# A Fourier and RG-LRU layer on one core: seven-product (Strassen) output projection for the last three position blocks, x put into PSUM for two others, and a new order of that stage

## The chip, the cores and the metric

The kernel runs on 1 core of one Trainium2 chip. The metric is the device time of one execution in microseconds. TensorE (PE) multiplies, VectorE (DVE) and ScalarE (ACT) work element by element, GpSimd (POOL) issues DMAs in this stage, and so does SyncE (SP), whose queue is in order. Before the change, three runs took 667.74, 668.42 and 664.72 us, the median is 667.74.

## The reference, cut to what matters

One layer of a diffusion backbone on 2048 positions of 1024 channels. The change is in the last step alone, `out_proj` with its gated residual and the final norm:

```python
def out_proj(y_f, g_f, y_l, g_l, w_out):
    y = jnp.concatenate([y_f * jax.nn.silu(g_f), y_l * jax.nn.silu(g_l)], axis=-1)
    return y @ w_out
...
        x = x + gate * out_proj(yf_x, gf_x, yl_x, gl_x, w_out[l])
    return rmsnorm(x, final_gain)
```

`y_f` comes from the Fourier group, `y_l` from the bidirectional recurrence, `g_f` and `g_l` are their gate paths. `gate` is one vector, so the kernel multiplies it into `w_out` once.

## The kernel before

All matrix products are made in three passes: each factor is split into a rounded part (hi) and the rest (lo), and `mm3` (L70 to L73) issues hi x hi, hi x lo and lo x hi into the same PSUM tile. A left factor is the stationary operand of a matmul, the weights are the moving one, so each matmul also loads its stationary tile (PEld).

The stages follow each other: input projection (string S1), Fourier transform and linear map (STEPS), gates and recurrence (S2), and the output projection (S3). Each string is a list of tokens, and its order is the order in which the instructions stand on PE, ACT and DVE (a manual schedule, L732). On SP and POOL the order is left to the scheduler. The last stage works on 8 blocks of 256 positions in the order 0, 3, 4, 7, 1, 2, 5, 6. The weights are in SBUF as `wo[k, n]`: 8 tiles k of 128 rows by 2 column halves n of 512, hi and lo. The tokens of a block b, with the Fourier half q = 0 and the recurrence half q = 1:

- D loads `g` and `yf` or `yl` from DRAM on SP (L946 to L954), A is silu(g) on ACT (L1001), P multiplies on DVE (L1008 for yf in two instructions of 512, L1010 for yl in one of 1024).
- J rounds to hi on ACT (L1015), K subtracts to lo on DVE (L1019); four tiles of 512 in a block.
- X loads x (`xr`, four buffers) on SP (L1055). m is a group of 4 k for position half t and column half n: 12 matmuls of 512 columns into `po` (four PSUM tiles).
- a adds `po` to x on DVE (L1077), b squares and sums on ACT (L1082), r takes the root on ACT (L1086), f is a reciprocal and the scaling with the final gain on DVE (L1090, L1091) and the store from POOL's queue (L1092). x's buffer is free for the next X when that store has ended.

A block without a special form is 2 x 2 x 8 products, 96 matmuls of 512 columns. The last half (Z6.1, `p3_last`) is cut into 512, 256 and 256 columns and is squared, scaled and stored in pieces, its halves from the queues of ACT and SP. The buffers of g, yf, yl and of the hi and lo tiles have the tag q4, 14 of them.

Of the kernel before, what the change touches and what calls it, by code (L numbers as in the profile page):

```python
# [52 lines left out]
def tile_layer(ctx, tc, xp, xnat, xt_in, ctxn, ctxt, w_ada, vec, bgate, fgain, w_in, w_g, w_four, w_gate, w_out,  # L53
# [997 lines left out]
    def p3_x(b):
        xs[b] = []
        for t in range(2):
            x = py.tile([P, D], F32, name=f"xr{b}_{t}", tag="xr", bufs=4)
            nc.sync.dma_start(x, xnat[256 * b + P * t:256 * b + P * t + P, :])  # L1055
            xs[b].append(x)
# [31 lines left out]
    def p3_scale(b, t):  # L1088
        o, st = xs[b][t], s3[b, t]
        nc.vector.reciprocal(out=st[:, 3:4], in_=st[:, 2:3])  # L1090
        nc.vector.scalar_tensor_tensor(out=o, in0=o, scalar=st[:, 3:4], in1=fg_bc, op0=ALU.mult, op1=ALU.mult)  # L1091
        nc.gpsimd.dma_start(out[256 * b + P * t:256 * b + P * t + P], o)  # L1092

    def p3_last(b, t):
        o = xs[b][t]
# [3 lines left out]
        for i, (n0, n1) in enumerate(((0, 512), (512, 768), (768, 1024))):  # L1099
            n, m0 = divmod(n0, 512)  # L1100
            po = ps3.tile([P, n1 - n0], F32, name=f"po{b}_{t}_{n0}", tag="po")
            for k in range(KD):
                p3_mms(po, b, t, n, k, m0, m0 + n1 - n0)
# [135 lines left out]
```

## Time and profile before

| | us |
|---|---|
| median of three runs | 667.74 |
| lowest, highest | 664.72, 668.42 |
| the profiled execution: time | 663.85 |
| its span | 661.7 |
| PE, DVE, ACT, POOL busy in the span | 651.6, 477.2, 402.9, 105.5 |
| block 4's first matmul, PE's last matmul (start) | 521.7, 655.60 |

The profiled execution's time is its span and 2.15 us around it. An engine's busy time says how much work it had, not whether anybody waited for it: that is read from the chain of waits and from the stretch in question. The duration of a matmul row is modelled and overlaps the next, so the pace of PE is read from the starts. The granted TensorE clock was 0.997 of full speed over the span.

### The profile page before, as it was taken

The numbers are of one execution on the slowest core, as the hardware profiler recorded it, in microseconds if no ns is written. First come the engines' busy times: TensorE is split into PE (matmuls) and PEld (weight loads), VectorE is DVE, ScalarE is ACT, GpSimd is POOL, SyncE is SP. The second block draws the span as 40 slices with busy tenths as digits, with TensorE's granted clock in tenths as the row PEclk, the third lists the DMA queues.
The fourth block names the chain that finished last, engine by engine and source line by source line (L and its number), as shares of the span: only waits on it lengthen the run. The fifth ranks groups of instructions, "written<-read, shape, count | busy, mean of one in ns | idle before, by whom it ended". The sixth has DMA issues, their size and how long they took to land.

```text
span 661.7 us, 10718 instructions
## 1 busy us (share of the span) xinstructions
PE 651.6 (98%) x4124; PEld 572.6 (87%) x4124; DVE 477.2 (72%) x771; ACT 402.9 (61%) x578; POOL 105.5 (16%) x170
## 2 busy tenths in 40 slices
PE   8999999999999999999999999999999999999996
PEld 8888888888988898998999999989988888888885
DVE  4768899877656775588699899879988455644513
ACT  5575877556644545959598696797643455543502
POOL 0000101031221204432212221131300000000000
PEclk9999999999999999999999999999999999999998
DMA  8996876539698776436344442251578677774211
GB/s 334 417 395 205 259 266 204 211 104 278 143 314 283 248 241 182 127 89 185 112 144 124 164 155 88 69 175 56 178 254 310 204 240 244 240 261 146 95 64 63
DMA packets 69884, 130.21 MB, mean 197 GB/s; under 512 B 7076, under 2 KB 39972, under 8 KB 69834
## 3 DMA queue, kind: packets, MB, share of 16 engines
q1 hardware_dynamic: 51066, 82.36, 37.9%
q0 software_dynamic: 12384, 39.00, 18.0%
q10 hardware_dynamic: 6384, 8.18, 4.0%
q8 instruction: 32, 0.52, 0.3%
q14 instruction: 18, 0.15, 0.1%
HBM read 91.24 MB, written 38.27 MB: 196 GB/s over the span
## 4 chain that ended last, share of the span: by engine, by line
PE 93%; DMA 3%; ACT 2%; DVE 1%; issue 1%; POOL 0%; SPq 0%; DVEq 0%; ACTq 0%; POOLq 0%
PE po L71 9%; PE pg L71 9%; PE po L72 9%; PE po L73 9%; PE pg L73 9%; PE pg L72 9%; PE pul L71 5%; PE pul L73 4%; PE pul L72 4%; PE ptt L71 2%; PE ptt L73 2%; PE ptt L72 2%; PE pl L72 2%; PE pl L73 2%; PE pl L71 2%; DMA yf_d<-ya 1%
## 5 line engine op out<-in xcount | busy, mean ns | idle before, releaser
L71 PE MATMUL pg<-hg,wg 128*128 128x256 f32 x512 | 144.2, 282 | 0.0
L73 PE MATMUL pg<-hg,wg 128*128 128x256 f32 x512 | 143.7, 281 | 0.0
L72 PE MATMUL pg<-hg,wg 128*128 128x256 f32 x512 | 143.5, 280 | 0.0
L71 PE MATMUL po<-wo,y 128*128 128x512 f32 (+1 forms) x264 | 102.4, 388 | 0.0
L72 PE MATMUL po<-wo,y 128*128 128x512 f32 (+1 forms) x264 | 102.3, 387 | 0.0
L73 PE MATMUL po<-wo,y 128*128 128x512 f32 (+1 forms) x264 | 102.3, 387 | 0.0
L71 PEld LDWEIGHTS pg<-hg,wg 128*128 128x128 f32 x512 | 96.3, 188 | 3.3 <-ACT g L852 1.2
L72 PEld LDWEIGHTS pg<-hg,wg 128*128 128x128 f32 x512 | 96.3, 188 | 0.7
L73 PEld LDWEIGHTS pg<-hg,wg 128*128 128x128 f32 x512 | 96.4, 188 | 0.0
L424 POOL DMA_DIRECT2D g_d<-gs x80 | 57.7, 723 | 135.5 <-DVE gs L758 63.2
L71 PEld LDWEIGHTS po<-wo,y 128*128 128x128 f32 x264 | 49.9, 189 | 11.0
L73 PEld LDWEIGHTS po<-wo,y 128*128 128x128 f32 x264 | 49.6, 188 | 11.2
L72 PEld LDWEIGHTS po<-wo,y 128*128 128x128 f32 x264 | 49.6, 188 | 10.7
L71 PE MATMUL pul<-hl,wu 128*128 128x512 f32 x124 | 49.9, 402 | 0.0
L1082 ACT ACTIVATE j<-xr 128x1024 bf16<-128x1024 f32 x15 | 15.9, 1057 | 55.3 <-DVE xr L1077 55.3
L73 PE MATMUL pul<-hl,wu 128*128 128x512 f32 x124 | 48.9, 395 | 0.0
L72 PE MATMUL pul<-hl,wu 128*128 128x512 f32 x124 | 48.8, 394 | 0.0
L852 ACT ACTIVATE g<-pl,vecs 128x1024 f32<-128x1024 f32 x32 | 35.5, 1116 | 13.5 <-PE pl L73 13.3
L287 ACT ACTIVATE h<-xt,sh,gn 128x512 f32<-128x512 f32 x31 | 25.2, 813 | 19.2 <-DVE gn L149 10.4
L71 PE MATMUL ptt<-wf,eo 128*128 128x260 f32 (+1 forms) x128 | 36.5, 285 | 0.0
L73 PE MATMUL ptt<-wf,eo 128*128 128x260 f32 (+1 forms) x128 | 36.3, 283 | 0.0
L72 PE MATMUL ptt<-wf,eo 128*128 128x260 f32 (+1 forms) x128 | 36.2, 283 | 0.0
(298 smaller groups left out, 1459.6 us busy)
## 6 DMA issues: line engine op xcount, KB each, us to landing
xt<-in_xt_dram SPq DMA_DIRECT2D x16, 512.0 KB, 5.2
blk<-in_w_ada_dram SPq DMA_DIRECT2D x16, 512.0 KB, 9.5
hr<-h_d SPq DMA_DIRECT2D x32, 256.0 KB, 3.7
xr<-in_xnat_dram SPq DMA_DIRECT2D x16, 512.0 KB, 3.7
g<-g_d SPq DMA_DIRECT2D x15, 512.0 KB, 5.5
out_dram<-xr POOLq DMA_DIRECT2D x15, 512.0 KB, 2.9
dm<-in_dct_dram POOLq DMA_DIRECT2D x12, 514.0 KB, 8.2
x<-in_xp_dram SPq DMA_DIRECT2D x12, 512.0 KB, 5.7
```

Source lines behind the costliest of these rows:

```text
L71: nc.tensor.matmul(out_, lh, rh, start=first, stop=False, skip_group_check=skip)
L72: nc.tensor.matmul(out_, lh, rl, start=False, stop=False, skip_group_check=skip)
L73: nc.tensor.matmul(out_, ll, rh, start=False, stop=last, skip_group_check=skip)
L287: nc.scalar.activation(out=h[:, 0:n], in_=x, func=AF.Identity, scale=g, bias=b)
L424: queue.dma_start(dst[:, :, row:row + s1 - s0], s[:, :, P * i - off + s0:P * i - off + s1])
L852: nc.scalar.activation(out=t[:, c0:c0 + cn], in_=pg[:, 0:cn], func=AF.Sigmoid, bias=vecs[:, q:q + 1])
L1082: nc.scalar.activation(out=junk, in_=xs[b][t], func=AF.Square, accum_out=s3[b, t][:, 0:1])
```

## The change

The output projection of blocks 2, 5 and 6 (`ST`) is made by the seven products of Strassen's method in Winograd's form. The y of a block is seen as 2 x 2 (position halves by Fourier and recurrence half), the weights as 2 x 2 (row halves by column halves). For each k of 4, four combinations of weight tiles are formed on the chip once, in float, and split into hi and lo: token Q (`t_raw`, DVE), H (`t_hi`, cast on ACT), L (`t_lo`, DVE). Per block S forms four combinations of y on DVE, h and l split seven left factors, p (`s_mm`) makes a product of 4 k, 12 matmuls of 512 columns, and q (`s_read`) adds a PSUM tile to a half of x, seven times (block 6: six of 512 and two of 256 columns, with its last product in two pieces, p6.8 and p6.9). Products 6, 5 and 3 are added onto the PSUM tile of product 1 after it has been read, product 4 onto that of product 7.

In blocks 7 and 1, token e (`p3_fill`) copies x into the PSUM tile on ACT, the matmuls add onto it without a start flag, token a is gone, and b and f read PSUM.

Besides: q4 has 6 buffers in place of 14; the pool of the stage ahead is closed before the projection's own pool is opened; x is loaded by halves (X b.t); from there on the order on SP and POOL is written by hand too. Both halves of block 6 are finished in pieces (`s_last`): the second half is scaled on ACT as a whole and stored from POOL, the first half last, its two column halves stored from ACT and SP. The tokens of S3 stand in a new order behind block 3's preparation.

```diff
-Q4 = 14
+Q4 = 6
+TR = 2
...
+    manual = tc.manual_schedule(engines={mybir.EngineType.PE, mybir.EngineType.Activation, mybir.EngineType.DVE,
+                                         mybir.EngineType.SP, mybir.EngineType.Pool})
...
             w[:, 0, m0:m1], w[:, 1, m0:m1], k == 0 and (b, t) not in filled, k == KD - 1, skip=True)
...
+    def p3_fill(b, t):
+        filled.add((b, t))
+        pos[b, t] = ps3.tile([P, D], F32, name=f"po{b}_{t}", tag="po")
+        nc.scalar.copy(pos[b, t], xs[b][t])
...
+    def t_raw(k, i):
+        if i != 2:
+            tr[k, i] = py.tile([P, 2, 512], F32, name=f"tr{k}_{i}", tag="tr", bufs=TR)
+        b11, b12, b21, b22 = ([r(wo[k + 4 * a, n][:, e, 0:512]) for e in range(2)] for a in range(2) for n in range(2))
+        w = tr[k, 1 if i == 2 else i]
+        if i % 2:
+            nc.vector.tensor_tensor(out=w, in0=r((wo[k, 1], wo[k + 4, 1])[i // 2][:, :, 0:512]),
+                                    in1=r(wo[k, i // 2][:, :, 0:512]), op=ALU.subtract)
+            nc.vector.tensor_tensor(out=w[:, 0], in0=w[:, 0], in1=w[:, 1], op=ALU.add)
+            return
+        o = w[:, int(i == 2)]
+        nc.vector.tensor_tensor(out=o, in0=(b22, b21)[i // 4][0], in1=tr[k, 1][:, i // 4], op=ALU.subtract)
+        nc.vector.tensor_tensor(out=o, in0=o, in1=(b22, b21)[i // 4][1], op=ALU.add)
...
+    def t_lo(k, i):
+        t = wt[k, i]
+        nc.vector.tensor_tensor(out=t[:, 1, 0:512], in0=tr[k, 1 if i == 2 else i][:, int(i == 2)], in1=r(t[:, 0, 0:512]),
+                                op=ALU.subtract)
...
+    def s_add(b, i):
+        a11, a12, a21, a22, s1 = (s_view(b, c) for c in (1, 2, 7, 4, 5))
+        o, x, y, op = {1: (s1, a21, a22, ALU.add), 2: (a11, s1, a11, ALU.subtract),
+                       3: (a21, a11, a21, ALU.subtract), 4: (a12, a12, a11, ALU.subtract)}[i]
+        nc.vector.tensor_tensor(out=o, in0=x, in1=y, op=op)
...
+    def s_mm(b, c):
+        p = {2: 2, 4: 1, 7: 1, 8: 3, 9: 4}.get(c, 0)
+        if c in (1, 2, 7, 8, 9):
+            pos[b, p] = ps3.tile([P, D], F32, name=f"po{b}_{p}", tag="po")
+        m0, m1, c = (0, 256, 3) if c == 8 else (256, 512, 3) if c == 9 else (0, 512, c)
+        o = pos[b, p][:, 0:m1 - m0]
+        t = yv[b, "s", c]
+        for k in range(4):
+            w = wo[k, 0] if c == 1 else wo[k + 4, c - 2] if c < 4 else wt[k, {4: 4, 5: 1, 6: 2, 7: 3}[c]]
+            mm3(o, t[:, 0, k], t[:, 1, k], w[:, 0, m0:m1], w[:, 1, m0:m1], (c in (1, 2, 7) or p > 2) and k == 0, k == 3, skip=True)
+
+    def s_read(b, i):
+        t, n, p = ((0, 0, 0), (0, 0, 2), (1, 0, 0), (1, 1, 0), (0, 1, 0), (1, 1, 1), (1, 0, 1),
+                   (0, 1, 0), (0, 2, 3), (0, 3, 4))[i]
+        w = 256 if i > 7 else 512
+        src = pos[b, p][:, 0:w]
+        o = xs[b][t][:, 512 + 256 * (n - 2) if i > 7 else 512 * n:][:, 0:w]
+        nc.vector.tensor_tensor(out=o, in0=o, in1=src, op=ALU.add)
...
+        if t:
+            nc.scalar.activation(out=q, in_=q, func=AF.Copy, scale=rs)
+            nc.gpsimd.dma_start(out[t0:t0 + P, :], q)
+            return
```

Three places in the order. First DVE behind the lo splits of block 7 (y_0_7, y_1_7): `tr` are raw combinations of weights, `wo` the weights, `xr` x, `po` PSUM, `s` the norm's scalars. Before:

```order
L1019 TENSOR_TENSOR y_0_7_5861<-g_7_5855,y_0_7_5861 128x512
L1019 TENSOR_TENSOR y_1_7_5864<-g_7_5855,y_1_7_5864 128x512
L1077 TENSOR_TENSOR xr_0_5693<-xr_0_5693,po_0_5867 128x1024
L1090 RECIPROCAL s_4_0_5917<-s_4_0_5917 128x1
L1091 SCALAR_TENSOR_TENSOR xr_0_5693<-xr_0_5693,s_4_0_5917,fg_bc 128x1024
```

After:

```order
L1023 TENSOR_TENSOR y_1_7_5898<-g_7_5820,y_1_7_5898 128x512
L1115 TENSOR_TENSOR tr_1_5920<-wo_1_5187,wo_0_5196 128x1024
L1117 TENSOR_TENSOR tr_1_5920<-tr_1_5920 128x512
L1103 RECIPROCAL s_3_1_5870<-s_3_1_5870 128x1
L1104 SCALAR_TENSOR_TENSOR xr_1_5590<-xr_1_5590,s_3_1_5870,fg_bc 128x1024
L1090 TENSOR_TENSOR xr_0_5865<-xr_0_5865,po_0_5830 128x1024
L1120 TENSOR_TENSOR tr_1_5920<-wo_1_5533,tr_1_5920 128x512
L1121 TENSOR_TENSOR tr_1_5920<-tr_1_5920,wo_1_5533 128x512
```

The combinations of weights stand between the sums and scalings of blocks 3 and 4, each reading what the one before it wrote.

Second DVE after the change at block 2's first reading (`t_2`, `t_3` are lo parts of combined weights, `s_2_...` with `g_2` a left factor of block 2); none of these stood in the kernel before:

```order
L1115 TENSOR_TENSOR tr_3_6368<-wo_1_5544,wo_1_5349 128x1024
L1117 TENSOR_TENSOR tr_3_6368<-tr_3_6368 128x512
L1169 TENSOR_TENSOR xr_0_6283<-xr_0_6283,po_0_6347 128x512
L1129 TENSOR_TENSOR t_2_6240<-tr_1_6184,t_2_6240 128x512
L1150 TENSOR_TENSOR s_2_6361<-g_2_6092,s_2_6361 128x512
L1103 RECIPROCAL s_1_0_6298<-s_1_0_6298 128x1
L1104 SCALAR_TENSOR_TENSOR xr_0_6031<-po_0_6071,s_1_0_6298,fg_bc 128x1024
```

Between the reading of product 1 and the scaling of block 1's first half stand the two lo splits for block 2's third product.

Third SP's queue around the loads of block 5 (`xr` of x, `g_5`, `yf`, `yl`). Before:

```order
L1055 DMA xr_0_6188<-in_xnat_dram 128x1024
L954 DMA g_5_6318<-g_d 128x4x256
L949 DMA yf_6320<-yf_d 128x4x128 x2
L1055 DMA xr_1_6190<-in_xnat_dram 128x1024
L954 DMA g_5_6336<-g_d 128x4x256
L951 DMA yl_6338<-yl_d 128x4x256
```

After:

```order
L1063 DMA xr_0_6283<-in_xnat_dram 128x1024
L1063 DMA xr_1_6363<-in_xnat_dram 128x1024
L956 DMA g_5_6422<-g_d 128x4x256
L951 DMA yf_6424<-yf_d 128x4x128 x2
L1063 DMA xr_0_6428<-in_xnat_dram 128x1024
L956 DMA g_5_6447<-g_d 128x4x256
L953 DMA yl_6449<-yl_d 128x4x256
```

Before, the loads of block 5 stand between those of block 2's x; after, both x loads of block 2 and the first one of block 5 stand ahead of the last g and yl of block 5.

## Rows read from the trace of the kernel before

**Rows 1.** The page's part 4, the chain that ended last, shares of the span.

```profile
PE 93%; DMA 3%; ACT 2%; DVE 1%; issue 1%; POOL 0%; SPq 0%; DVEq 0%; ACTq 0%; POOLq 0%
```

**Rows 2.** Stretches: length, busy (instructions) of PE, PEld, DVE, ACT, POOL; clock, DMA share, GB/s.

```profile
521.70:588.60 66.90, 66.90 (x289) 54.19 (x288) 37.42 (x47) 35.76 (x52) 4.79 (x9) 1.00 0.67 227
588.60:655.90 67.30, 67.27 (x313) 55.32 (x311) 28.60 (x38) 23.66 (x38) 3.19 (x6) 1.00 0.31 111
655.90:661.70 5.80, 0.00 (x0) 0.00 (x0) 1.50 (x4) 1.52 (x4) 0.00 (x0) 0.67 0.23 90
```

**Rows 3.** Timeline of PE near the end: start, duration, line, shapes.

```profile
642.13 0.40 PE L73 MATMUL po<-wo,y 128*128 128x512 f32 x1
...
647.70 0.39 PE L73 MATMUL po<-wo,y 128*128 128x512 f32 x1
...
650.02 0.28 PE L71 MATMUL po<-wo,y 128*128 128x256 f32 x1
...
652.85 0.28 PE L71 MATMUL po<-wo,y 128*128 128x256 f32 x1
...
655.60 0.28 PE L73 MATMUL po<-wo,y 128*128 128x256 f32 x1
```

**Rows 4.** Groups by line and form, 520 to 661.7: busy us, mean ns | idle before.

```profile
L1091 DVE SCALAR_TENSOR_TENSOR xr<-xr,s,fg_bc 128x1024 f32<-128x1024 f32 x15 | 19.3, 1285 | 0.5
L1077 DVE TENSOR_TENSOR xr<-xr,po 128x1024 f32<-128x1024 f32 x14 | 17.0, 1216 | 19.7 <-PE po L73 19.7
L1082 ACT ACTIVATE j<-xr 128x1024 bf16<-128x1024 f32 x15 | 15.9, 1057 | 55.3 <-DVE xr L1077 55.3
L1019 DVE TENSOR_TENSOR y<-g,y 128x512 fp32r<-128x512 f32 x20 | 12.9, 689 | 7.1 <-ACT y L1015 7.1
L1015 ACT CAST y<-g 128x512 fp32r<-128x512 f32 x20 | 11.4, 618 | 13.5 <-DVE g L1010 6.5 <-issue 5.6 <-DVE g L1008 1.4
...
L1008 DVE TENSOR_TENSOR g<-g,yf 128x512 f32<-128x512 f32 x10 | 6.5, 690 | 4.4 <-ACT g L1001 4.4
L1010 DVE TENSOR_TENSOR g<-g,yl 128x1024 f32<-128x1024 f32 x5 | 6.1, 1225 | 1.6 <-ACT g L1001 1.6
...
L1062 ACT ACTIVATE j<-xr 128x512 bf16<-128x512 f32 x1 | 0.6, 631 | 3.6 <-DVE xr L1060 3.6
```

**Rows 5.** Timeline of all engines behind the last matmul: start, duration, instruction.

```profile
655.91 0.42 DVE L1060 TENSOR_TENSOR xr<-xr,po 128x256 f32<-128x256 f32 x1 [1.45 <-PE po L73]
...
656.43 0.42 ACT L1062 ACTIVATE j<-xr 128x256 bf16<-128x256 f32 x1 [2.35 <-DVE xr L1060]
656.75 0.19 ACT L1062 ACTIVATION_READ_ACCUMULATOR j<-xr 128x1 f32 x1
656.97 0.29 ACT L1110 ACTIVATE s<-s,bias 128x1 f32<-128x1 f32 x1
657.29 0.16 DVE L1112 RECIPROCAL bias<-s 128x1 f32<-128x1 f32 x1 [0.50 <-ACT s L1110]
```

**Rows 6.** Timeline of DVE where block 4's yl arrives: start, duration, [idle <-releaser].

```profile
515.49 1.22 DVE L1010 TENSOR_TENSOR g<-g,yl 128x1024 f32<-128x1024 f32 x1 [3.50 <-DMA yl<-yl_d]
517.40 1.29 DVE L1019 TENSOR_TENSOR y<-g,y 128x512 fp32r<-128x512 f32 x2 [0.69 <-ACT y L1015]
```

**Rows 7.** Timeline of SP's queue at the loads for block 5: start, duration.

```profile
580.12 0.35 SPq L1055 DMA_DIRECT2D xr<-in_xnat_dram  x1
...
581.12 0.50 SPq L951 DMA_DIRECT2D yl<-yl_d  x1
```

**Rows 8.** DMA issues, 580 to 640 us: count, KB each, median us to landing.

```profile
yl<-yl_d SPq DMA_DIRECT2D x2, 512.0 KB, 5.8
```

**Rows 9.** The stores of the output, 520 to 662 us: issue ns, then landing.

```profile
L1092 POOL DMA_DIRECT2D out_dram<-xr x15: 532/532/534, 524.4 to 649.2; - x15
...
DMA to landing us min/median/max: 2.0/2.9/7.3
```

**Rows 10.** The loads of yl, 480 to 662 us, issue to landing.

```profile
DMA to landing us min/median/max: 5.7/6.8/9.3
```

More of the change, by code (lines that the diff above doesn't have):

```diff
@@ L491, in tile_layer @@
     gate_bc = gpool.tile([P, D], F32, name="gate_bc")
-    p2s = tail
+    p2s = ExitStack()
     p2 = p2s.enter_context(tc.tile_pool(name="p2", bufs=1, side="right", reuse_waits="tile"))
@@ L956, in tile_layer @@
     first = {}
+    ST = (2, 5, 6)
     def p3_first_load(b):
@@ L1034, in tile_layer @@
         ops[x[0]](*(int(c) for c in x[1:].split(".")))
-    xs, pos, s3 = {}, {}, {}
+    xs, pos, s3, filled = {}, {}, {}, set()
     ops.update({"D": p3_load, "A": p3_silu, "P": p3_mul, "J": p3_hi, "K": p3_lo})
@@ L1047, in tile_layer, with p3_x @@
     lst.close()
+    p2s.close()
+    manual.__exit__(None, None, None)
+    manual = tc.manual_schedule(engines={mybir.EngineType.PE, mybir.EngineType.Activation, mybir.EngineType.DVE,
+                                         mybir.EngineType.SP, mybir.EngineType.Pool})
+    manual.__enter__()
     py = pool["y"] = tail.enter_context(tc.tile_pool(name="py", bufs=1, side="right", reuse_waits="tile"))
     fg_bc = py.tile([P, D], F32, name="fg_bc", tag="fg")
[L1051 to L1056, printed above, removed]
+    def p3_x(b, t):
+        tag, n = ("tt", 12) if b == XT else ("xr", 4)
+        x = py.tile([P, D], F32, name=f"xr{b}_{t}", tag=tag, bufs=n)
+        nc.sync.dma_start(x, xnat[256 * b + P * t:256 * b + P * t + P, :])
+        xs.setdefault(b, []).append(x)
     def p3_add(b, t, n0, n1, po, acc):
@@ L1066, in p3_mms @@
         mm3(po, yt[:, 0, k % 2, P * t:P * t + P], yt[:, 1, k % 2, P * t:P * t + P],
-            w[:, 0, m0:m1], w[:, 1, m0:m1], k == 0, k == KD - 1)
+            w[:, 0, m0:m1], w[:, 1, m0:m1], k == 0 and (b, t) not in filled, k == KD - 1, skip=True)
     def p3_group(b, t, n, kk):
@@ L1081, in p3_square @@
         junk = py.tile([P, D], BF16, name=f"j3_{b}_{t}", tag="j3", bufs=1)
-        nc.scalar.activation(out=junk, in_=xs[b][t], func=AF.Square, accum_out=s3[b, t][:, 0:1])
+        nc.scalar.activation(out=junk, in_=pos[b, t] if (b, t) in filled else xs[b][t], func=AF.Square, accum_out=s3[b, t][:, 0:1])
     def p3_sqrt(b, t):
@@ L1090, in p3_scale @@
         nc.vector.reciprocal(out=st[:, 3:4], in_=st[:, 2:3])
-        nc.vector.scalar_tensor_tensor(out=o, in0=o, scalar=st[:, 3:4], in1=fg_bc, op0=ALU.mult, op1=ALU.mult)
+        nc.vector.scalar_tensor_tensor(out=o, in0=pos[b, t] if (b, t) in filled else o, scalar=st[:, 3:4], in1=fg_bc, op0=ALU.mult, op1=ALU.mult)
         nc.gpsimd.dma_start(out[256 * b + P * t:256 * b + P * t + P], o)
-    def p3_last(b, t):
-        o = xs[b][t]
-        st = py.tile([P, 4], F32, name=f"s3_{b}_{t}", tag="s3", bufs=4)
-        q = py.tile([P, D], F32, name="q_last", tag="q4", bufs=Q4)
-        bias = py.tile([P, 2], F32, name="bias", tag="bias", bufs=1)
[L1099 to L1103, printed above, removed]
-            p3_add(b, t, n0, n1, po, st[:, i:i + 1])
+    wt, tr = {}, {}
@@ new lines, in t_hi, with s_view @@
+    def t_hi(k, i):
+        t = wt[k, i] = wtile(f"t{k}_{i}", "Wu") if i == 3 else py.tile([P, 2, 512], F32R, name=f"t{k}_{i}", tag="tt", bufs=12)
+        nc.scalar.copy(t[:, 0, 0:512], tr[k, 1 if i == 2 else i][:, int(i == 2)])
+    def t_lo(k, i):
+        t = wt[k, i]
+        nc.vector.tensor_tensor(out=t[:, 1, 0:512], in0=tr[k, 1 if i == 2 else i][:, int(i == 2)], in1=r(t[:, 0, 0:512]),
+                                op=ALU.subtract)
+    def s_view(b, c):
+        gf, gl, m = gms[b, 0][0], gms[b, 1][0], gms[b, 0][1]
+        return {1: gf[:, :, 0:P], 2: gl[:, :, 0:P], 3: gl[:, :, 0:P], 4: gl[:, :, P:256], 5: m[:, :, 0, :],
+                6: gf[:, :, 0:P], 7: gf[:, :, P:256]}[c]
@@ new lines, in s_add, with s_hi @@
+    def s_add(b, i):
[3 more added lines that the diff above has]
+        nc.vector.tensor_tensor(out=o, in0=x, in1=y, op=op)
+    def s_hi(b, c):
+        tl = gms[b, 0 if c in (1, 5, 6, 7) else 1][2]
+        t = yv[b, "s", c] = tl(f"s{c}", [P, 2, 4, P], F32R)
+        nc.scalar.copy(t[:, 0], s_view(b, c))
@@ new lines, in s_lo @@
+    def s_lo(b, c):
+        t = yv[b, "s", c]
+        nc.vector.tensor_tensor(out=t[:, 1], in0=s_view(b, c), in1=r(t[:, 0]), op=ALU.subtract)
+    def s_mm(b, c):
[4 more added lines that the diff above has]
+        o = pos[b, p][:, 0:m1 - m0]
+        t = yv[b, "s", c]
+        for k in range(4):
+            w = wo[k, 0] if c == 1 else wo[k + 4, c - 2] if c < 4 else wt[k, {4: 4, 5: 1, 6: 2, 7: 3}[c]]
+            mm3(o, t[:, 0, k], t[:, 1, k], w[:, 0, m0:m1], w[:, 1, m0:m1], (c in (1, 2, 7) or p > 2) and k == 0, k == 3, skip=True)
@@ new lines, in s_read, with s_last @@
+    def s_read(b, i):
[5 more added lines that the diff above has]
+        nc.vector.tensor_tensor(out=o, in0=o, in1=src, op=ALU.add)
+    def s_last(b, i):
+        t, i = divmod(i, 4)
+        o, t0 = xs[b][t], 256 * b + P * t
+        if i == 0:
+            fin[t] = (py.tile([P, 4], F32, name=f"s3_{b}_{t}", tag="s3", bufs=4),
+                      py.tile([P, D], F32, name=f"q_last{t}", tag="q4", bufs=Q4),
+                      py.tile([P, 2], F32, name=f"bias{t}", tag="bias", bufs=2))
+        st, q, bias = fin[t]
+        rs = bias[:, 0:1]
+        if i < 3:
+            n0, n1 = ((512, D), (0, 512), None) [i] if t else ((0, 512), (512, 768), (768, D))[i]
+            junk = py.tile([P, D], BF16, name=f"j3_{b}_{t}_{n0}", tag="j3", bufs=1)
+            nc.scalar.activation(out=junk[:, n0:n1], in_=o[:, n0:n1], func=AF.Square, accum_out=st[:, i:i + 1])
@@ L1105, in p3_last @@
             nc.vector.tensor_tensor(out=q[:, n0:n1], in0=o[:, n0:n1], in1=fg_bc[:, n0:n1], op=ALU.mult)
-            if i == 1:
-                nc.vector.tensor_tensor(out=bias[:, 0:1], in0=st[:, 0:1], in1=st[:, 1:2], op=ALU.add)
-                nc.vector.tensor_scalar(out=bias[:, 1:2], in0=bias[:, 0:1], scalar1=1.0 / D, scalar2=EPS,
+            if i + t == 1:
+                if t == 0:
+                    nc.vector.tensor_tensor(out=st[:, 0:1], in0=st[:, 0:1], in1=st[:, 1:2], op=ALU.add)
+                nc.vector.tensor_scalar(out=bias[:, 1:2], in0=st[:, 0:1], scalar1=1.0 / D, scalar2=EPS,
```

12 lines of the change are left out of this document (7 added, 5 removed).

## The prediction

> **What bounds the kernel now.** I read the page's chain first, then the projection stage cut into stretches, then single rows. The chain gives TensorE 93% of the span [rows 1]. From 521.7 us, where block 4's matmuls begin, PE is busy 66.90 of 66.90 us, then 67.27 of 67.30; DVE is busy 37.42 and 28.60 us there, ACT 35.76 and 23.66 [rows 2]. So PE never waits, the other engines have 40% to 60% of their time free, and this stage ends when its matmuls are through. The granted clock is 1.00 in both stretches, the 2.4 GHz level. The duration of a matmul row is modelled; the pace is in the starts: 642.13 to 647.70 holds 24 starts of 512 columns, 0.232 us each, and 650.02 to 652.85 holds 24 of 256 columns, 0.118 us each [rows 3]. After PE's last row comes a tail: add at 655.91, square, root, reciprocal, scaling, store; the span ends at 661.7, 5.8 us after PE [rows 2, 5].
>
> The sum is made against the profiled run, 663.85 us with its span of 661.7; the median of the three runs is 667.74, 3.9 us more. The difference in time is worked out in the trace and put on the median.
>
> **What is removed on PE.** A block by the plain product is 2 halves x 2 column halves x 8 k x 3 = 96 matmuls of 512 columns; by seven products of 4 k x 3 it is 84. Blocks 2 and 5 lose 12 each. Block 6 before is 72 of 512 and 48 of 256; after, 72 of 512 and 24 of 256. Removed: 24 x 0.232 + 24 x 0.118 = 5.57 + 2.83 = **8.4 us** [rows 3]. That is all PE time, and PE is the bound, so 8.4 is the gain if no product waits. The filled blocks 7 and 1 keep their 96 matmuls: putting x into PSUM saves PE nothing, it spares DVE four additions of 1.216 us and gives ACT four copies.
>
> **What is added on DVE, and whether it hides.** Weight combinations: for each of 4 k two instructions of 1024 elements, six of 512 and four lo splits of 512, so 8 x 1.225 + 40 x 0.69 = 37.4 us. Combinations of y: 12 x 0.69 = 8.3. Lo splits of the seven left factors instead of four tiles: 9 x 0.69 = 6.2. Readings of PSUM in three blocks: 21 x 0.69 + 2 x 0.42 = 15.3 against 7.6 for the sums before. Minus 4 x 1.216 of the filled blocks. Sum: +54.7 us [rows 4, 5]. DVE then has 66.0 + 54.7 = 121 us of work where PE has 134.2 - 8.4 = 125.8 us: 96%. So a total says "hidden, just"; what decides is each place where PE waits for DVE in order.
>
> The tightest is the start of block 2's third product, the first with a built weight. DVE's queue from the multiplication by block 4's yl (515.49, the transfer that ended there set it before and still does [rows 6]) to the first reading of block 2 holds 93 instructions: 17 of 1024, 60 of 512, 8 scalings of 1.285 and 8 reciprocals of 0.16 [rows 4]: 20.8 + 41.4 + 10.3 + 1.3 = 73.8 us, so it gets there at 589.3. Back to back, two of 512, those at 517.40, took 1.29 together [rows 6], which takes up to 7 us off where neighbours are independent; the raw combinations are not, each reads the one before. The reading can start when block 2's first product is through: 521.7 + 288 x 0.232 = 588.6, plus 12 x 0.232 = 591.4. Spare: **2.1 us** at full durations, some 9 at pitch. Behind it reading and two lo splits, 3 x 0.69, end at 593.5, and PE wants the third product at 588.6 + 24 x 0.232 = 594.2. So 0.7 to spare there at most, whatever DVE did earlier, and the same pattern (read a tile, then add the next product onto it) comes back at two more products of each block; I price all of these at 0 to 0.5 us and take 0.2.
>
> ACT gains 16 casts of weights, 9 of left factors and four fills: 25 x 0.618 + 4 x 1.06 = 19.7 us on 59.4 [rows 2, 4]; at about 80 of 126 us it is not the next bound. A fill stands on PE's path only if its x comes late. The latest is block 7's second half: its buffer is free when block 3's second half is scaled and stored, which DVE's queue reaches some 20 us after 515.5; with 2.9 for the store, even 5.8 for the load and 1.06 for the fill it is there at 546, and PE wants it at 521.7 + 144 x 0.232 = 555.1. If that cover of 9 us were gone, PE would wait for whatever is missing; I take 0.
>
> **Loads: the second tight place.** Q4 goes from 14 buffers to 6, so g, yf and yl come later, and SP's queue is in order: block 5's x load waits for the store of block 1's first half out of the same buffer, and g and yl of block 5's LRU half are queued behind it. Before, block 5's yl was issued at 581.12, 1.00 us behind the x load ahead of it [rows 7], some 30 us before block 5's matmuls, which began after four blocks of 22.3. After: that half is scaled on DVE after block 2's third product is prepared: 593.5 + 0.16 + 1.285 = 594.9. The store lands 2.9 us after its issue (median), yl's issue follows 1.00 us after x's, yl lands after 5.8 [rows 8]: 604.6. Multiplication 1.22 and one lo split 0.69: 606.5. Block 5's third matmul, the first that reads the lo part, wants it at 588.6 + 86 x 0.232 = 608.6: **2.1 us** to spare. The store's landing spread is 2.0 to 7.3 [rows 9] and yl's 5.7 to 9.3 [rows 10]; at the worst of both the wait is 4.4 + 3.5 - 2.1 = 5.8 us, at the best none. This stretch moved 111 GB/s before against 227 earlier [rows 2], so I take the medians and 0.5 us for the risk.
>
> **The tail.** The last product is now two pieces of 256 columns, as before, and the closing chain is the same. But ACT also scales the other half (1024 elements, about 1.06) right ahead of the last squares: the second to last product ends 24 x 0.118 = 2.8 us before PE's end; add 0.69, square 0.63 + 0.19, root 0.29, reciprocal 0.16, copy 1.06, square 0.42 + 0.19 pass 3.4 to 3.6 us, where the last square could start 0.5 us after PE's end. So +0.3 us; 0 if the rows overlap, +1.9 if that half's store (512 KB, from POOL) takes the 7.3 us of the slowest one [rows 5, 9].
>
> **Sum.** -8.4 + 0.3 (tail) + 0.2 (products) + 0.5 (block 5) = **-7.4 us**: 656.4 on the profiled run, **660.3** on the median.
>
> **The rivals.**
> (a) Block 5's loads come late, the landings nearer their slow ends: +2 to +5.8 us more, 662.3 to 666. For it: the margin is 2.1 us, less than the spread of one store. Against: medians in just this stretch.
> (b) POOL's stores are held up by a DVE that is busy all the time. In the trace POOL's issue took 532 to 534 ns in all 15 cases [rows 9], many beside DVE work, so nothing shows it. If each store waited for one running DVE instruction (1.285 at most [rows 4]), block 5's chain loses 1.3 of its 2.1 us and nothing is seen; with a landing 2 us over the median it is 1.2 us late, 661.5. The Trainium skill ("SBUF — State Buffer", section "Who interferes with whom") says that a DVE instruction with two SBUF inputs blocks a GpSimd instruction that reads SBUF, which speaks against packing DVE beside POOL's stores; by the 15 equal issue rows this case has no sign of it.
> (c) **Slower**: the new DVE forms cost more than the rows they are priced by. No row shows a two-input instruction on weight tiles read as plain float, or one updating a 2x512 tile in place. Of the 73.8 us up to block 2's first reading 38.8 are new forms (8 of 1024, 42 of 512). At 1.27 times the price they use up spare time and gain (10.5 - 2.1 = 8.4); from 1.35 the kernel is slower by over 0.5%; at 1.5 the wait is 19.4 - 2.1 = 17.3 us: 677. Against: strided views cost nothing extra before (L1008 takes every second row of g, 690 ns; L1019 689 [rows 4]).
> (d) The change does not do what it says for PE: products on combined tiles run at less than the plain pace, or PE is held by something that 48 matmuls fewer do not shorten. Then 667.7 + 0.3 = 668. Against it: same instruction shapes, and PE is 100% busy.
>
> **How the numbers follow.** Forecast 0.66, (a) 0.15, (b) 0.05, (c) 0.08, (d) 0.06. This kernel can be told from no change beyond about 0.5%, so faster means under 664.4 and slower over 671.1. Forecast and (b) are faster, and 0.09 of (a): 0.80. The rest of (a), (d) and a little of (c): 0.13. The rest of (c): 0.07. The forecast's own band is 659.3 (no wait, no tail cost) to 662; the three runs before lie 3.0 us under and 0.7 over their median, so down to 656.3. Leaving out (c), (d) and the worst of (a): **656 to 665**.
>
> **What would show it.** 24 matmuls of 512 and 24 of 256 fewer, at 0.232 and 0.118; PE's last row near 647.4 (plus waits) in place of 655.9; DVE over 90% busy from 522 to 647; each of blocks 4, 7 and 1 still 22.3 us, blocks 2, 5 and 6 near 19.5. A wait of PE at the third product of block 2 would speak for DVE's queue, one at the start of block 5 behind a late yl for (a), DVE rows over 0.75 us at 512 for (c). I am wrong if PE waits more than 2 us in all or if the tail passes 6.5 us.

## The result, and the profile after

The changed kernel took 656.49 us (median of four runs, 656.03 to 656.83) against 666.23 for the kernel before (663.94 to 668.42): a ratio of 0.985, 95% interval 0.981 to 0.989. It is 1.5% faster, 9.7 us between the medians, and the interval is clear of one. A second comparison on one chip gave 656.15 against 665.20, ratio 0.985 (0.982 to 0.988). The prediction was 660.3 us with a range of 656 to 665; the time lies in the range, at its low edge. The profiled execution took 656.83 us with a span of 655.1: the span is 6.6 us shorter than before, and the time outside it is 1.7 us in place of 2.15.

The answer of the trace to "what does PE wait for" is empty between 480 us and the end, as it was before. So the first thing to read is the pace and the length of the projection stage, from its first `po` matmul to its last. The timeline of PE after, at both ends:

```profile
478.29 0.39 PE L73 MATMUL po<-wo,y 128*128 128x512 f32 x1
...
648.40 0.28 PE L75 MATMUL po<-wo,s 128*128 128x256 f32 x1
```

170.11 us. Before, the last stood at 655.60 [rows 3] and the first here:

```profile
477.12 0.39 PE L71 MATMUL po<-wo,y 128*128 128x512 f32 x1
```

That makes 178.48 us. The stage is 8.37 us shorter; 8.4 was the sum. The span splits so: the stages ahead of the projection, which the change doesn't touch, were 1.17 us longer in this execution, the stage 8.37 shorter, the tail behind PE's last start 6.70 in place of 6.10. 1.2 - 8.4 + 0.6 = -6.6.

The same stretches as in [rows 2], block by block (columns: length, busy and instructions of PE, PEld, DVE, ACT, POOL, then clock, DMA share, GB/s):

```profile
521.70:544.00 22.30, 22.30 (x97) 18.05 (x96) 21.56 (x31) 17.82 (x26) 2.66 (x5) 1.00 0.91 308
544.00:566.30 22.30, 22.30 (x97) 18.07 (x96) 19.43 (x28) 16.54 (x23) 0.53 (x1) 1.00 0.58 198
566.30:588.60 22.30, 22.30 (x97) 18.07 (x96) 20.35 (x28) 14.12 (x22) 1.07 (x2) 1.00 0.22 81
588.60:608.10 19.50, 19.50 (x85) 15.78 (x84) 15.67 (x24) 6.90 (x10) 1.06 (x2) 1.00 0.62 216
608.10:627.60 19.50, 19.50 (x86) 15.77 (x85) 17.81 (x28) 12.14 (x18) 1.06 (x2) 1.00 0.63 198
627.60:647.20 19.60, 19.60 (x92) 16.12 (x91) 16.00 (x27) 9.02 (x18) 1.06 (x2) 1.00 0.26 99
```

PE is full in each, at the upper clock. DVE, 37.42 of 66.90 and 28.60 of 67.30 us before, is now busy 110.8 of 125.5 us: 88%. It has become nearly as full as PE, and still PE never waits for it. The new DVE forms in the groups by line and form (busy us, mean ns | idle before):

```profile
L1150 DVE TENSOR_TENSOR s<-g,s 128x512 fp32r<-128x512 f32 x18 | 12.3, 685 | 0.0
...
L1129 DVE TENSOR_TENSOR t<-tr,t 128x512 fp32r<-128x512 f32 x16 | 10.5, 685 | 1.4 <-ACT t L1125 1.4
L1115 DVE TENSOR_TENSOR tr<-wo,wo 128x1024 f32<-128x1024 f32 x8 | 9.8, 1222 | 0.1
...
L1121 DVE TENSOR_TENSOR tr<-tr,wo 128x512 f32<-128x512 f32 x8 | 5.5, 693 | 0.3
...
```

1222 and 685 to 693 ns: the prices of [rows 4]. And the places that the prediction called tight, in the timelines of DVE and of SP's queue:

```profile
590.18 0.69 DVE L1117 TENSOR_TENSOR tr<-tr 128x512 f32<-128x512 f32 x1
592.78 0.69 DVE L1169 TENSOR_TENSOR xr<-xr,po 128x512 f32<-128x512 f32 x1 [1.91 <-PE po L75]
...
594.78 1.29 DVE L1104 SCALAR_TENSOR_TENSOR xr<-po,s,fg_bc 128x1024 f32<-128x1024 f32 x1
...
607.32 1.23 DVE L1014 TENSOR_TENSOR g<-g,yl 128x1024 f32<-128x1024 f32 x1 [0.85 <-DMA yl<-yl_d]
608.46 0.69 DVE L1150 TENSOR_TENSOR s<-g,s 128x512 fp32r<-128x512 f32 x1
```

```profile
599.32 0.35 SPq L1063 DMA_DIRECT2D xr<-in_xnat_dram  x1
599.76 0.39 SPq L956 DMA_DIRECT2D g<-g_d  x1
600.24 0.46 SPq L953 DMA_DIRECT2D yl<-yl_d  x1
```

At block 2's first reading (592.78) DVE had been waiting 1.91 us for PE. At block 5 it is DVE that waits, 0.85 us for yl, which landed 7.0 us after its issue; the lo split behind it ends at 609.15, and PE starts the matmul that reads it at 609.81: 0.66 us to spare in this trace.

### The profile page after: what moved, and what is told of

The parts are those of the page before. It is cut to its first block, busy times and chain, and to the rows that moved or that the text cites. A ratio compares the mean times of both kernels' runs of the same rounds, so it can differ in the third digit from the quotient of the medians.

```text
span 655.1 us, 10772 instructions
## 1 busy us (share of the span) xinstructions
PE 643.2 (98%) x4076; PEld 565.0 (86%) x4076; DVE 524.9 (80%) x853; ACT 423.9 (65%) x612; POOL 105.5 (16%) x170
## 4 chain that ended last, share of the span: by engine, by line
PE 86%; ACT 5%; DMA 3%; DVE 3%; issue 2%; POOL 0%; SPq 0%; ACTq 0%; DVEq 0%; POOLq 0%
PE po L74 9%; PE po L73 9%; PE po L75 9%; PE pg L73 8%; PE pg L75 8%; PE pg L74 7%; PE pul L73 5%; PE pul L75 4%; PE pul L74 4%; PE ptt L73 2%; PE ptt L75 2%; PE ptt L74 2%; PE pl L74 2%; PE pl L75 2%; PE pl L73 2%
## 5 line engine op out<-in xcount | busy, mean ns | idle before, releaser
L73 PE MATMUL po<-wo,y 128*128 128x512 f32 x160 | 63.1, 394 | 0.0
L74 PE MATMUL po<-wo,y 128*128 128x512 f32 x160 | 63.1, 394 | 0.0
L75 PE MATMUL po<-wo,y 128*128 128x512 f32 x160 | 63.1, 394 | 0.0
L73 PEld LDWEIGHTS po<-wo,y 128*128 128x128 f32 x160 | 30.3, 189 | 7.0
L75 PEld LDWEIGHTS po<-wo,y 128*128 128x128 f32 x160 | 30.0, 188 | 7.2
L74 PEld LDWEIGHTS po<-wo,y 128*128 128x128 f32 x160 | 30.0, 188 | 6.8
L810 DVE SCALAR_TENSOR_TENSOR v<-up,vecs,v 128x1284 f32<-128x1284 f32 (+1 forms) x24 | 34.1, 1419 | 1.9 <-ACT v L803 1.4
```

What stands on the lines that cost most here:

```text
L73: nc.tensor.matmul(out_, lh, rh, start=first, stop=False, skip_group_check=skip)
L74: nc.tensor.matmul(out_, lh, rl, start=False, stop=False, skip_group_check=skip)
L75: nc.tensor.matmul(out_, ll, rh, start=False, stop=last, skip_group_check=skip)
L810: nc.vector.scalar_tensor_tensor(out=v[:, 0:w], in0=up[:, j:j + w], scalar=cw[:, j:j + 1], in1=v[:, 0:w], op0=ALU.mult, op1=ALU.add)
```

## The experiments

The stage and the tail of each kernel are read from PE's starts as above; times are medians.

| kernel | stage | tail | first po matmul | time | ratio to before, interval |
|---|---|---|---|---|---|
| before | 178.48 | 6.10 | 477.12 | 665.20 (17 runs) | |
| changed, again (e1) | 170.10 | 6.70 | 478.00 | 656.15 | 0.985 (0.982 to 0.988) |
| before, fewer matmuls (e2) | 170.07 | 6.09 | 476.94 | 656.51 | 0.986 (0.984 to 0.989) |
| changed, matmuls back (e3) | 178.48 | 6.68 | 481.14 | 665.62 | 1.001 (0.999 to 1.003) |
| tail on DVE (e4) | 170.10 | 7.02 | 477.88 | 656.75 | 0.986 (0.983 to 0.988) |
| no fills (e5) | 172.19 | 6.63 | 480.68 | 657.65 | 0.991 (0.988 to 0.994) |
| DVE padded (e6) | 176.49 | 6.64 | 477.57 | 663.07 | 0.997 (0.995 to 1.000) |
| scaling 6 us later (e7) | 174.58 | 6.66 | 480.56 | 660.73 | 0.995 (0.993 to 0.996) |
| one store less (e8) | 170.10 | 6.41 | 477.69 | 656.17 | 0.987 (0.986 to 0.989) |
| scaling 1.8 us later (e9) | 171.96 | 6.67 | 477.87 | 657.33 | 0.988 (0.985 to 0.991) |
| e9 with yl first (e10) | 170.08 | 6.62 | 479.20 | 657.85 | 0.989 (0.986 to 0.992) |
| tail cut 384 and 128 (e11) | 170.65 | 6.63 | 478.82 | 657.78 | 0.989 (0.985 to 0.993) |

e1 to e4 were compared with one set of runs of the kernel before (665.20), e5 to e8 with a second (664.81), e9 to e11 with a third (666.01).

**e1, the change once more.** No edit.

> The changed kernel once more, beside the kernel before on the same chip. The two traces so far differ by 6.6 us in span: the projection stage (first po matmul to last) went from 178.48 to 170.11 us (-8.4), the stages ahead of it lasted 1.2 us longer in that one run, the tail behind the last matmul 0.6 us longer (6.1 to 6.7). Theory A: what repeats is -8.4 + 0.6 = -7.8 us, and the 1.2 us ahead of the stage is spread between runs; so -7 to -8.5 us when both run side by side. Theory B: the change also shortens or steadies something ahead of the projection, and the difference of the first medians (-9.7) repeats: -9 to -11 us.

Stage and tail repeat to 0.01 us. The difference between the medians is 9.0 us, by the interval 8.2 to 11.8. That is more than the 7.8 of stage and tail: the medians fall at the near edge of theory B, and the interval reaches into both. What the other 1.2 us are is taken up under "The median" below.

**e2, only the matmuls taken away.** In the kernel before:

```diff
+        kd = 4 if b in (2, 5) and t and n else KD
-        for k in range(kk, kk + 4):
+        for k in range(kk, min(kk + 4, kd)):
...
-            for k in range(KD):
+            for k in range(4 if i else KD):
```

> The kernel before with the same number and shapes of matmuls taken away as the change takes away, and nothing else: the last group of 12 in the second half of blocks 2 and 5, and half of the 48 matmuls of 256 columns in block 6's last half (these sums are left out). Theory A: matmuls are the whole gain: stage 178.5 - 8.4 = 170.1 us, time -8.4 us against the kernel before, and PE waits for nothing. The changed kernel then lies 0.3 to 1 us above it, by its longer tail. Theory B: the order, the buffers and the fills bring a part of their own: this kernel gains less than 7 us.

PE's first and last `po` matmul in e2:

```profile
476.94 0.39 PE L71 MATMUL po<-wo,y 128*128 128x512 f32 x1
...
647.01 0.28 PE L73 MATMUL po<-wo,y 128*128 128x256 f32 x1
```

170.07 us, the stage of the changed kernel, with nothing of its order, buffers, fills or DVE work; the time is that of the changed kernel too, 656.51 beside 656.15.

**e3, the matmuls put back.** In the changed kernel's `s_mm`:

```diff
+        if c == 1:
+            for a, z in ((0, 256), (256, 512)) if b == 6 else ((0, 512),):
+                for k in range(4):
+                    mm3(pos[b, p][:, 512 + a:512 + z], t[:, 0, k], t[:, 1, k], wo[k + 4, 1][:, 0, a:z], wo[k + 4, 1][:, 1, a:z], k == 0, k == 3, skip=True)
```

> The changed kernel with the saved matmuls put back as idle work: behind the first product of blocks 2 and 5 twelve more of 512 columns, behind that of block 6 twenty-four of 256, into the unused half of the same PSUM tile, read by nobody. Theory A: +8.4 us against the changed kernel, so 0.3 to 1 us above the kernel before. Theory B (a part of the gain is not matmuls): +8.4 still, but the kernel stays 1.5 us or more below the kernel before.

PE's first and last `po` matmul in e3:

```profile
481.14 0.39 PE L73 MATMUL po<-wo,y 128*128 128x512 f32 x1
...
659.62 0.28 PE L75 MATMUL po<-wo,s 128*128 128x256 f32 x1
```

178.48, the stage before to the hundredth, and a time 0.4 us above the kernel before. The longer tail says 0.6, and the shorter time outside the span takes 0.4 off. e2 and e3 from both sides: the matmul count is the whole difference in the stage, and DVE's added work (44.8 us of busy time, 54.7 by the prediction's full durations) cost the stage nothing as placed.

**e4, e8 and e11, the tail.** e4 scales block 6's second half on DVE, e8 leaves its store out, e11 is e4 with another cut (the readings and squares of that product are cut to match, which is not shown):

```diff
-            nc.scalar.activation(out=q, in_=q, func=AF.Copy, scale=rs)
+            nc.vector.tensor_scalar_mul(q, q, rs)
```

```diff
-            nc.gpsimd.dma_start(out[t0:t0 + P, :], q)
             return
```

```diff
-        m0, m1, c = (0, 256, 3) if c == 8 else (256, 512, 3) if c == 9 else (0, 512, c)
+        m0, m1, c = (0, 384, 3) if c == 8 else (384, 512, 3) if c == 9 else (0, 512, c)
```

> The changed kernel with one line changed: block 6's second half is scaled by DVE (one instruction of 1024) in place of ACT. In the trace the ACT scaling ran 648.00 to 649.05 and the last two squares waited behind it, while DVE idled 0.81 us before the last sum at 648.71. If the longer tail comes from that queue: tail 6.7 to about 6.2 us, time -0.4 to -0.5 us against the changed kernel. If the tail is set by the landing of the last stores: no change. If the DVE scaling lasts over 0.9 us it delays the last sum and gives back part.

> The changed kernel without the store of block 6's second half (that part of the output is left out). The tail behind PE's last matmul is 6.70 us in both traces of the changed kernel, 6.10 before; ACT's scaling of 1.15 us for that half is still there. Theory A (the queue on ACT: the last squares wait behind that scaling): the tail stays at 6.5 to 6.7. Theory B (the store of 512 KB holds up the last two stores or the end): the tail falls to 6.1 to 6.3.

> The changed kernel with block 6's second half scaled by DVE and the last product cut into 384 and 128 columns in place of 256 and 256. The DVE scaling alone left the tail at 7.0 us: the last square waited for the multiplication by the gain that stands ahead of it on DVE, and the stores landed later. With 128 columns the last sum, square and multiplication are some 0.1 us shorter each. Theory A: tail 6.4 to 6.8, stage 170.1 plus at most 0.3 for narrower matmuls, no difference in time that can be told. Theory B (the instruction chain sets the end): tail 6.2 or less.

The end of the changed kernel, in the timeline of all engines:

```profile
648.00 1.15 ACT L1194 ACTIVATE q_last<-q_last,bias 128x1024 f32<-128x1024 f32 x1 [0.29 <-DVE bias L1192]
648.71 0.42 DVE L1169 TENSOR_TENSOR xr<-xr,po 128x256 f32<-128x256 f32 x1 [0.81 <-PE po L75]
...
649.05 0.40 ACT L1183 ACTIVATE j<-xr 128x256 bf16<-128x256 f32 x1
...
649.58 0.42 ACT L1183 ACTIVATE j<-xr 128x256 bf16<-128x256 f32 x1
...
651.16 0.34 SPq L1200 DMA_DIRECT2D out_dram<-q_last  x1
651.40 0.36 ACTq L1198 DMA_DIRECT2D out_dram<-q_last  x1
```

The last store's issue, in the kernel before and in e8:

```profile
658.24 0.36 ACTq L1115 DMA_DIRECT2D out_dram<-q_last  x1
```

```profile
650.79 0.36 ACTq L1197 DMA_DIRECT2D out_dram<-q_last  x1
```

The last square waits behind ACT's scaling and the square before it, as predicted. These issues part the tail in two. From PE's last start to the last issue it is 2.64 us before, 3.00 in the changed kernel and in e8: ACT's queue costs 0.36. From there to the end of the span it is 3.46, 3.70 and 3.41: the store of the second half costs 0.24 to 0.29. So e8's tail of 6.41, half of the extra 0.6 back, lies between the two theories because each is right for a half. With the scaling off ACT (e4) the last square started behind DVE's multiplication instead, the last stores were issued only 0.07 us sooner after PE, the end came 4.09 us behind the last issue, and the tail was 7.02; why the end is that late there is not shown. e11's tail is 6.63, and its stage 0.55 longer, since 384 and 128 columns together take longer than twice 256 (PE's starts in e11):

```profile
646.20 0.34 PE L73 MATMUL po<-wo,s 128*128 128x384 f32 x1
646.37 0.33 PE L74 MATMUL po<-wo,s 128*128 128x384 f32 x1
...
649.36 0.28 PE L74 MATMUL po<-wo,s 128*128 128x128 f32 x1
649.47 0.28 PE L75 MATMUL po<-wo,s 128*128 128x128 f32 x1
```

None of the three can be told from the changed kernel in time: the intervals of the ratios overlap.

**e5, without the fills.** In the string of tokens e7.0, e7.1, e1.0 and e1.1 are gone, and a sum stands ahead of each square:

```diff
-... e7.0 ... e7.1 ... b7.0 ... b7.1 ... b1.0 ... b1.1
+... a7.0 b7.0 ... a7.1 b7.1 ... a1.0 b1.0 ... a1.1 b1.1
```

> The changed kernel without its fills: blocks 7 and 1 are added to x by DVE as before the change (four additions of 1.216 us back on DVE, four copies off ACT), all else the same. In the changed kernel's trace DVE arrives at block 2's first reading 1.9 us before PE lets it start, and the two lo splits behind it end 1.2 us before PE's third matmul wants them. Theory A (a place decides, not the total): 4.9 - 1.9 - 1.2 = 1.8 us of waiting on PE at block 2's third product, less if DVE's waits for ACT (1.3 and 1.4 us) shrink because ACT has less to do: 0 to 1.8 us, +0 to +1.8 us in time. Theory B (DVE's total decides, fills are a main part of the gain): +4 us or more.

The stage is 2.09 us longer. PE's waits in e5:

```profile
PE po L73 <- ACT t L1125: 1.2, 1, 1.2
PE po L75 <- DVE s L1150: 0.4, 1, 0.4
```

Both at block 2's third product: first the hi part of a combined weight from ACT, which itself waits for DVE, then the lo split of the left factor. 4.9 us more on DVE cost 2.1, a little over the 1.8 of theory A: the place decides. The fills are part of what lets the products hide, worth 2 us of the 8.4.

**e6, more DVE work.** In `t_lo`:

```diff
-        nc.vector.tensor_tensor(out=t[:, 1, 0:512], in0=tr[k, 1 if i == 2 else i][:, int(i == 2)], in1=r(t[:, 0, 0:512]),
+        for _ in range(2):
+            nc.vector.tensor_tensor(out=t[:, 1, 0:512], in0=tr[k, 1 if i == 2 else i][:, int(i == 2)], in1=r(t[:, 0, 0:512]),
```

> The changed kernel with each of the 16 lo splits of combined weights made twice, the second time over the same result: 16 x 0.61 to 0.69 = 9.8 to 11.0 us more on DVE, 13 of them (8 to 9 us) before block 2's first reading. It measures the room that rival (c) of the prediction spoke of. Theory A: spare of 1.9 us at the reading, 1.2 behind it and up to 2.7 us of waits for ACT are eaten first; then PE waits, 3.5 to 7 us in all, nearly all of it at block 2's third to fifth products, and the time is 3.5 to 7 us longer. Theory B: DVE has more room than the queue shows (waits for ACT and PE move): under 2 us.

The stage is 6.38 us longer than the changed kernel's. The list of PE's waits names only 3.1 us of it:

```profile
PE po L73 <- ACT t L1125: 2.5, 1, 2.5
PE po L75 <- DVE s L1151: 0.6, 1, 0.6
```

Most of the rest is the clock. The stretches behind the wait (the third column from the right is the granted clock):

```profile
596.00:600.00 4.00, 2.03 (x4) 1.25 (x5) 3.93 (x7) 0.62 (x1) 0.00 (x0) 0.66 0.99 330
600.00:604.00 4.00, 4.00 (x10) 3.06 (x10) 3.16 (x6) 0.00 (x0) 0.53 (x1) 0.50 0.33 135
604.00:608.00 4.00, 4.00 (x18) 3.26 (x17) 3.97 (x7) 1.50 (x2) 0.00 (x0) 0.98 0.81 260
```

From 600 to 604 PE is fully busy, at 0.50, the 1.2 GHz level, and starts a matmul each 0.43 us in place of 0.232: ten intervals from 599.75 to 604.02, 1.9 us lost without any wait in the list. In e5, where PE waited 1.2 and 0.4 us, the clock stayed at 1.00:

```profile
598.00:602.00 4.00, 2.49 (x10) 1.76 (x11) 3.96 (x7) 0.63 (x2) 0.15 (x1) 1.00 0.86 281
```

**e7, e9 and e10, the loads of block 5.** In the string of tokens f1.0, the scaling of block 1's first half, moves behind the last lo split of combined weights (e7) or by three lo splits only (e9); e10 is e9 with D5.1, the loads of g and yl, ahead of X5.0:

```diff
-... l2.6 f1.0 p2.6 L3.3 l2.7 l2.5 p2.7 q2.2 D5.0 L3.1 X5.0 ...
+... l2.6 p2.6 L3.3 l2.7 l2.5 p2.7 q2.2 D5.0 L3.1 f1.0 X5.0 ...
```

```diff
-... l2.6 f1.0 p2.6 L3.3 l2.7 l2.5 p2.7 q2.2 D5.0 L3.1 X5.0 ... D5.1 ...
+... l2.6 p2.6 L3.3 l2.7 l2.5 f1.0 p2.7 q2.2 D5.0 D5.1 L3.1 X5.0 ...
```

> The changed kernel with the scaling of block 1's first half moved down DVE's queue, behind the last lo split of combined weights: about 5 us later. Its store frees the buffer of block 5's first x, and g and yl of block 5 stand behind that load on SP. In the changed kernel's trace yl landed 7.1 us after its issue and the lo split that needs it ended 0.66 us before the matmul that reads it. Theory A (that chain is the second tight place): scaling ends near 601.1 instead of 596.1, yl is issued near 605, lands at 610.8 to 612.1, and PE waits 2.9 to 4.2 us at block 5's first product; the time is as much longer. Theory B (loads hide it): no wait, same time.

The size came near (stage +4.5, time 4.4 us over the changed kernel's 656.3, for 2.9 to 4.2), the mechanism did not come at all, so the size is luck. PE's waits in e7 hold one row, and it is not at block 5:

```profile
PE po L73 <- DVE xr L1104: 2.9, 1, 2.9
```

That is block 2's fourth product. It takes over the PSUM tile of block 1's first half, and since that half is filled, its scaling reads PSUM: until f1.0 is done the tile is not free. PE was then late enough at block 5 for yl. Most of the other 1.6 us are again matmuls 0.43 us apart behind the wait, at a granted clock of 0.50. So e7 said nothing on yl, and e9 was made to.

> The changed kernel with the scaling of block 1's first half moved only three lo splits down DVE's queue: 1.8 us later, ending near 597.9. That is before block 2's fourth product takes over the PSUM tile which this scaling reads (598.2 in the changed kernel's trace), so the PSUM tile should not hold PE, as it did when the scaling moved by 6 us. What is left is the chain store, block 5's x load, yl behind it on SP. The changed kernel had 0.66 us to spare there. Theory A: PE waits 0.3 to 1.3 us at the first product of block 5, at the matmul that reads the lo part, by yl's landing of 5.8 to 7.1 us. Theory B: the chain has more room than the trace shows: no wait at block 5.

PE's waits in e9:

```profile
PE po L75 <- DVE s L1150: 1.0, 1, 1.0
PE po L73 <- DVE xr L1104: 0.2, 1, 0.2
```

and two of DVE's waits ahead of them:

```profile
556.25 0.16 DVE L1103 RECIPROCAL s<-s 128x1 f32<-128x1 f32 x1 [3.78 <-ACT s L1099]
...
609.26 1.23 DVE L1014 TENSOR_TENSOR g<-g,yl 128x1024 f32<-128x1024 f32 x1 [2.81 <-DMA yl<-yl_d]
```

The third matmul of block 5, the one that reads the lo part, waits 1.0 us for the split that waits for yl (1.2 lost by the starts): 1.9 us later on SP (yl issued at 602.12) minus 0.66 of room. The 0.2 us at the PSUM tile were not expected to be there any more, and the edit is not all of it. DVE was late in this trace ahead of the edited place: it did not wait for PE at block 2's first reading, which it reached 0.5 us after PE would have let it start, where it had 1.4 to 1.9 us to spare in seven other traces with the same code up to there (the changed kernel, e1, e4, e7, e8, e10, e11). One place where it lost time is the wait at 556.25: 3.78 us for ACT, 1.29 in the changed kernel, behind the fill of block 7's second half, for whose x ACT had waited 4.23 us, 3.06 in the changed kernel. So of the 2.3 us by which the scaling is later, counted from the stage's start, 1.8 are the edit and 0.5 are this trace's.

> The kernel with the 1.8 us later scaling, and on SP's queue g and yl of block 5 moved ahead of block 5's x load, so that they no longer stand behind the store. Theory A: yl is issued 4 us or more earlier than in the changed kernel (600.24), no wait at block 5's start, stage 170.1 us. Theory B: yl is held by its buffer, not by its place in the queue: it is issued no earlier than 599 and the wait stays.

Here SP issues

```profile
592.49 1.33 SPq L953 DMA_DIRECT2D yl<-yl_d  x1
```

nearly ten us sooner than in e9, DVE no longer waits for yl, PE waits for nothing, and the stage is 170.08 us with the later scaling in place. DVE has its 1.91 us at block 2's first reading again, and with it the 0.2 us at the PSUM tile is gone. The chain store, x load, yl is shown by making it and by taking it away. The times of e9 and e10 (657.33 and 657.85) don't tell them apart; stage and waits do.

## Why the prediction was right, point by point

- **PE's 8.4 us.** Right to 0.03 us, and e2 and e3 show that nothing else makes the stage shorter. Counting removed starts at their start-to-start pace was enough.
- **DVE hides it.** Right, though the total was mis-sized: 121 us put busy time (66.0 before) and full durations (54.7) together, 110.8 were busy. Independent neighbours overlap at the pace of the pair in [rows 6] (four of 512 in 2.49 us at 518.35 after), and the total left that out. The reading counts of the sum hold: block 6 has seven of 512 and two of 256 columns, not six and two as the section on the change says. At the place itself 2.1 us to spare were predicted at block 2's first reading and 1.91 came, in part by luck, since errors cancel: DVE waited 4.4 us on the way there (1.24 for PE, 0.42, 1.29 and 1.42 for ACT), which the sum did not have, overlap gave back 3.4, DVE began 0.59 us later and PE 1.17. The wait of 1.29 comes from a fill: the prediction looked at fills on PE's path only, but a fill that waits for x holds up what stands behind it on ACT, and DVE waits for that. The 0.2 us priced for the products were none.
- **Block 5's loads.** The chain was right: scaling ending 594.9 plus the 1.17 of later start is 596.07, measured 594.78 + 1.29 = 596.07, and yl was issued 4.17 us behind it for 3.9. What varies is yl's landing. 5.8 was taken from two issues of a quieter stretch [rows 8]; the profiled execution of the changed kernel had 7.0, so 0.66 us to spare in place of 2.1. In the other traces with this order of loads block 5's yl landed after 5.6 to 6.2 us in eight (5.8 in e1, the same kernel) and after 7.0 in e9. So 5.8 was the usual case, 0.66 us is the room that a late landing leaves, and in such a trace the 0.5 us set aside were escaped by little.
- **A constraint that the prediction did not have.** Filling keeps a PSUM tile until the half is scaled, where before the sum freed it. e7 met it. In the changed kernel it leaves 2.1 us (f1.0 ends at 596.07, product four starts at 598.2).
- **The tail.** +0.3 predicted, +0.6 measured. The term for ACT's queue came out: 0.36 up to the last issue, with a scaling of 1.15 us, not 1.06. The store of 512 KB, put at nothing but for a slow landing, took the other 0.24 to 0.29 (e8).
- **Rival (b)**, POOL's stores held up by DVE: in 14 stores beside a DVE that is 88% busy the issue took what it took before [rows 9]:

```profile
L1105 POOL DMA_DIRECT2D out_dram<-xr x14: 532/532/534, 523.7 to 643.1; - x14
```

- **Rival (c)**, dearer DVE forms: prices equal within 1%. e6 tests the sum behind it: 8 to 9 us of its work stand ahead of block 2's first reading, less 2.1 to spare makes 5.8 to 6.9, and 6.4 came. The size came out, the make-up did not. The sum left out that the clock falls behind a wait (1.9 us), and also that DVE's own waits ahead of that reading can shrink, here from 4.4 to 0.6 us.
- **Its signs of being wrong.** PE waits for nothing, where 2 us were allowed. The tail, limited to 6.5, is near: 6.4 counted from the end of PE's last row, as the prediction counts its 5.8, and 6.7 from its start. DVE was to be over 90% busy and was 88%.
- **The median.** Here the prediction was off most: 660.3 against 656.5. Its base, 667.74 of three runs, lies 2.5 us above the later 665.2, and that 656.5 is still in the range is owed to the range's lower end, which takes in the spread of those three runs. Stage and tail give -7.8; the medians of e1 say -9.0 (interval 8.2 to 11.8). Of the 1.2 us between them 0.4 lie outside the span: time less span is 2.08 to 2.21 us in the 47 runs of the kernel before and e2 that list both, and 1.73 to 1.85 in all 63 of the changed kernel and its variants. That goes with something in the change other than the matmuls, since e2 has the longer and e3 the shorter; what it is stays open. The rest lies ahead of the stage. What stands there is the same code in all kernels and varies: the first `po` matmul stands between 476.94 and 481.14 in thirteen traces. Where it is latest (e3, e5, e7, e10), PE waited 1.4 to 2.1 us in the recurrence stage for one copy by ACT, and in the nine others it did not; the waits of e3 ahead of the projection, longest first, and the stretch around the first of them, then the same stretch in the changed kernel:

```profile
PE pc L73 <- ACT gs L760: 2.1, 1, 2.1
```

```profile
250.00:300.00 50.00, 47.92 (x350) 44.26 (x349) 31.56 (x40) 31.03 (x35) 20.24 (x28) 0.97 0.44 130
```

```profile
250.00:300.00 50.00, 50.00 (x379) 46.38 (x379) 33.35 (x42) 33.70 (x38) 20.22 (x28) 1.00 0.44 132
```

By the spans, the projection began at 478.5 us in the median of e1's 17 runs of the kernel before and at 477.6 in its four of the changed one, 0.9 us apart, which with the 7.8 and the 0.4 makes up the difference. That this part differed by chance is likely but not shown; both kinds of kernel have late runs (up to 481.5 us in those 17, up to 483.8 in e3). Whether the change also makes that wait rarer stays open: no run tells it.

## What to carry to other kernels

Where PE is full and starts at an even pace, a gain is the number of matmuls taken away times that pace, and it arrives whole as long as each product's inputs are ready in the order of the queues: sum the feeding engine's queue up to each deadline, not over the stage. Walk every buffer that a moved step holds, PSUM tiles among them, since the tile that a later reader keeps can stop PE before the data that one was watching. And put loads that PE needs ahead of loads that wait for a store: in an in-order queue that moved the issue 9.6 us forward and cost the stage nothing (e10 against e9). Read a margin from several traces: the same load landed after 5.6 to 7.0 us in ten traces, and the same reading had 1.9 us to spare or none.

## What the runs showed of the hardware that was not expected

- Behind PE waits of 2.5 and 2.9 us (e6, e7) the granted clock was 0.50 for some us, and matmuls of 512 columns started 0.43 us apart in place of 0.232; behind waits of 1.0 to 1.2 us (e5, e9) it stayed at 1.00. A wait's length alone does not tell which comes: behind the recurrence stage's wait of 2.1 us in e3 and 2.0 in e5 the clock was 0.50 and 0.55 for the 2 us from 256 and 255 us, behind 2.0 in e7 it stayed at 1.00. A wait cost up to twice what the list of waits showed: 3.1 listed, 6.4 lost in e6.
- A matmul of 128 columns started 0.111 us after the one ahead, one of 256 after 0.118, of 384 after 0.175, of 512 after 0.232, each with its own stationary tile. Below 256 columns a narrower matmul saved next to nothing.
- Four independent DVE additions or subtractions of 512 took 2.49 us, 0.60 from start to start at a duration of 0.685; where each reads what the one before wrote, 0.725.
